# Own buffers for the group norm's inverse root, and the inversion's masked copies moved behind both chunk halves

## The chip, the cores and the metric

The kernel runs on one core of a Trainium2 chip. The metric is the device time of one execution in microseconds (us), given as the median of several runs. TensorE appears as PE (its weight loads as PEld), VectorE as DVE, ScalarE as ACT, GpSimd as POOL and SyncE as SP.

## The reference, cut to what matters

One decoder block of width 2048 over 512 positions in float32. A normalised input goes through one wide projection. A part of its columns feeds RWKV-7 time mixing (16 heads of 64), a part windowed attention, a part two gates. Both branches are projected, gated, summed and projected back; a gated convolution network of width 5632 follows. The change lies in the time mixing:

```python
h = rms_norm(x, norm1_g[l])
z = h @ w_in[l]
...
kk = kk / jnp.maximum(jnp.sqrt(jnp.sum(kk * kk, axis=-1, keepdims=True)), 1e-12)
...
def step(state, inp):
    r_t, k_t, v_t, w_t, ka_t, kb_t = inp
    sa = jnp.einsum('bhvk,bhk->bhv', state, ka_t)
    state = (state * w_t[:, :, None, :] + sa[..., None] * kb_t[:, :, None, :]
             + v_t[..., None] * k_t[:, :, None, :])
    y = jnp.einsum('bhvk,bhk->bhv', state, r_t)
    return state, y
...
mu = jnp.mean(y, axis=-1, keepdims=True)
var = jnp.mean(jnp.square(y - mu), axis=-1, keepdims=True)
y = ((y - mu) * lax.rsqrt(var + GN_EPS)).reshape(B, S, RW_DIM)
```

## The kernel before, in words

The wide projection is made in tiles of 128 columns. For each tile `project` takes 16 slices of the inner dimension with three matmuls each (lines 255, 256 and 257: high and low parts of input and weight), so a tile is 48 matmuls of 128x512 into a PSUM tile called `acc`. Weights come in four slices at a time: SP loads `raw` (line 237), ACT rounds it to `whi` (line 240), DVE makes the rest `wlo` (line 241). There are four buffers of each. These matmuls depend on nothing but weights, so they serve as filling for everything else on PE.

The 16 RWKV heads are worked on as 8 pairs. For a pair, `early` projects k, r and v and prepares them: it squares k, sums it per head on PE (line 327), takes an inverse root of those sums with `rsqrt_small` (lines 185 to 200, tiles `rq0` to `rq2`), transposes the result (line 330), copies it to `rsT` (line 332), sends it to DRAM and back as a row spread over partitions (`rsd`, line 334, and `rsb`, line 338, both on SP's queue), and multiplies k by it (line 552, `kk`). Beside this it makes the decay (lines 558 to 568) and the bonus (lines 584 to 593; line 591 is a matmul on PE that needs `lw` of line 589).

`late` then does the recurrence in 8 chunks of 64 positions. Lines 603 to 606 write the operands `BKK` and `BAR`, line 623 multiplies them, and lines 627 to 647 build what the inversion of a triangular 64x64 matrix starts from, in two halves `g` of four chunks each: a 2x2 start `X`, the matrix `AI` as a high part (ACT, line 209) and a low part (DVE, line 210), and two masked copies of `AI` called `BT` (line 647). Five levels follow on PE (lines 671 and 672; first with `AI`, then with `BT`). Then the chain runs through the chunks one after another: `psG` on PE (line 729), its copy `GY` on DVE (730), `psU` on PE (732), its two half copies `UV` on ACT (733) and DVE (734), `psS` on PE (738), the new state `SV` on DVE (742). The group norm ends it: sums, then `rsqrt_small` again (line 762) with the same two sets of buffers `rq`, and a product (line 763). `final` transposes the result (line 770), adds the bonus and stores it.

The program calls `late(p)`, `early(p + 1)`, `final(p)` and three gate tiles of the wide projection for each pair. The order that the engines get is made by a scheduler: it walks a heap of ready instructions by priority and by estimated times, and an instruction whose tile has no free buffer has to wait for it. Each engine then executes its list in order.

Of the kernel before, what the change touches and what calls it, by code (L numbers as in the profile page):

```python
# [8 lines left out]
F32 = mybir.dt.float32  # L9
# [9 lines left out]
P = 128  # L19
S = 512  # L20
NT = S // P
HD = 64
# [5 lines left out]
GN_EPS = 64e-5  # L28
# [106 lines left out]
def block_kernel(ctx: ExitStack, tc: tile.TileContext, d: Dims, a: dict, out: bass.AP):  # L135
# [47 lines left out]
    def col(nm, i=0):  # L183
        return pcol[:, PR[nm] + i : PR[nm] + i + 1]

    def rsqrt_small(pl, ss, scale, eps, mx=None):
        n = ss.shape[-1]
        tl = [pl.tile([P, 8], F32, name=f"rq{i}", tag=f"rq{i}", bufs=2)[:, :n] for i in range(3)]
        v, y, t = tl
        if mx is not None:  # L190
            dve.tensor_scalar(v, ss, mx, None, op0=ALU.max)
        else:
            dve.tensor_scalar(v, ss, scale, eps, op0=ALU.mult, op1=ALU.add)
        dve.tensor_scalar(t.bitcast(I32), v.bitcast(I32), 1, None, op0=ALU.logical_shift_right)
        dve.tensor_scalar(y.bitcast(I32), t.bitcast(I32), -1, 0x5F3759DF, op0=ALU.mult, op1=ALU.add)
        dve.tensor_scalar(v, v, -0.5, None, op0=ALU.mult)
        for _ in range(3):
            dve.tensor_tensor(t, y, y, op=ALU.mult)
            dve.tensor_tensor(t, t, v, op=ALU.mult)
            dve.scalar_tensor_tensor(y, t, 1.5, y, op0=ALU.add, op1=ALU.mult)  # L200
        return y
# [6 lines left out]
    def split(hi, lo, src, pin=free):  # L208
        pin(act.activation(hi, src, AF.Copy))
        pin(dve.tensor_tensor(lo, src, hi.bitcast(F32) if hi.dtype == F32R else hi, op=ALU.subtract))  # L210
# [67 lines left out]
    if True:  # L278
# [3 lines left out]
        with tc.tile_pool(name="x0_ps", bufs=6, space=PSUM) as ps0:  # L282
            ssum = p0.tile([P, NT], F32, name="ssum")
            HT = NT // 2
            for h in range(2):
                for t in range(h * HT, (h + 1) * HT):
                    sq = p0.tile([P, d.D], F32, name="sqx", tag="sqx", bufs=1)
                    act.activation(sq, xt[t], AF.Square, accum_out=ssum[:, t : t + 1])
                r = rsqrt_small(p0, ssum[:, h * HT : (h + 1) * HT], 1.0 / d.D, RMS_EPS)
                for t in range(HT):  # L290
                    dve.tensor_scalar(xt[h * HT + t], xt[h * HT + t], r[:, t : t + 1], None, op0=ALU.mult)
            first = {d.c_ka: [load_w(zt[d.c_ka][:, k0 : k0 + 4]) for k0 in range(0, min(NK, 12), 4)]}
            for h in range(2):
                hs = slice(h * HT * P, (h + 1) * HT * P)
                for k in range(NK):
                    ps = ps0.tile([P, HT * P], F32, name="ps_x", tag="x")
                    for t in range(HT):
                        pe.transpose(ps[:, t * P : (t + 1) * P], xt[h * HT + t][:, k * P : (k + 1) * P], ident)
                    g = col("n1g", k)
                    act.activation(xhi[:, k, hs], ps, AF.Identity, scale=g)  # L300
                    dve.scalar_tensor_tensor(xlo[:, k, hs], ps, g, xhi[:, k, hs].bitcast(F32), op0=ALU.mult, op1=ALU.subtract)  # L301
# [40 lines left out]
        with ExitStack() as pt:  # L342
# [16 lines left out]
            def qk_norm(acc, gain, dst, then=lambda: None):  # L359
                z = ap_.tile([P, S], F32, name="zq", tag="zq", bufs=3)  # L360
                dve.tensor_scalar(z, acc, gain, None, op0=ALU.mult)
                sq = ap_.tile([P, S], F32, name="sqq", tag="sqq", bufs=2)
                act.activation(sq, acc, AF.Square)
                ps = small()
                head_stats(ps, sq)
                rs = rsqrt_small(ap_, ps[:, 0 : 2 * NT], 1.0 / HD, RMS_EPS)
                rb = head_rows(ap_, small(), rs, bufs=2)
                finish()
                unscaled.append((dst, z, rb, then))
# [38 lines left out]
            for g in range(NHK):  # L408
# [7 lines left out]
                for n in range(NT):  # L416
# [15 lines left out]
                    st = ap_.tile([P, 4, GQ], F32, name="st", tag="st", bufs=2)  # L432
                    mx, es, den, rc = (st[:, i] for i in range(4))
# [33 lines left out]
        with ExitStack() as pr:  # L467
# [3 lines left out]
            wk = pr.enter_context(tc.tile_pool(name="wk", bufs=1, reuse_waits="tile"))  # L471
# [17 lines left out]
            def bulk():  # L489
                return blk.tile([P, S], F32, name="bulk", tag="bulk")  # L490
# [38 lines left out]
            def r3(ap, c=C):  # L529
                return ap.rearrange("p (n c) -> p n c", c=c)  # L530
# [5 lines left out]
            def early(p):  # L536
# [11 lines left out]
                ps = bulk()  # L548
                head_stats(ps, sq)
                rs = rsqrt_small(wk, ps[:, 0 : 2 * NT], None, None, mx=1e-24)  # L550
                rb = head_rows(wk, bulk(), rs, "lg")
                dve.tensor_tensor(kk, kk, rb, op=ALU.mult)
# [43 lines left out]
            def late(p, st):  # L596
# [17 lines left out]
                HN = NCH // 2  # L614

                def mb(nm, n, h=None):
                    m = K[nm] if h is None else K[nm][h[0] : h[1]]
                    return m.unsqueeze(1).to_broadcast([m.shape[0], n, m.shape[-1]])
# [11 lines left out]
                for g in range(2):  # L630
                    ns = slice(g * HN, (g + 1) * HN)
                    for h, (lo, hi) in enumerate(HV):
                        own = AB[lo:hi, ns, h]
                        (dve.tensor_copy if h else act.copy)(BX[lo:hi, ns, lo:hi], own)
                        dve.tensor_tensor(tt[lo:hi, ns], own, mb("m1", HN, (lo, hi)), op=ALU.mult)
                    dve.tensor_tensor(tt[:, ns], tt[:, ns], mb("istack", HN), op=ALU.add)
                    split(X[:, 0, ns], X[:, 1, ns], tt[:, ns])
                    ps = bulk().rearrange("p (n c) -> p n c", c=P)
                    for j in range(HN):
                        pe.transpose(ps[:, j], BX[:, g * HN + j], ident)  # L640
                    for h, (lo, hi) in enumerate(HV):
                        (dve.tensor_copy if h else act.copy)(BX[lo:hi, ns, lo:hi], tt[lo:hi, ns])
                    at_ = wk.tile([P, HN, P], F32, name="at_", tag="at_")
                    dve.scalar_tensor_tensor(at_, ps, SG, mb("idsg", HN), op0=ALU.mult, op1=ALU.add)
                    split(AI[:, 0, ns], AI[:, 1, ns], at_)
                    for i in range(2):
                        dve.tensor_tensor(BT[:, i, ns], AI[:, i, ns], mb("t1bd", HN), op=ALU.mult)
                for g in range(2):
                    ns = slice(g * HN, (g + 1) * HN)
# [76 lines left out]
                for n in range(NCH):  # L726
# [17 lines left out]
                    if n % HN == HN - 1:  # L744
                        ns = slice(n + 1 - HN, n + 1)
# [9 lines left out]
                st = wk.tile([P, 2, NCH], F32, name="st", tag="st")  # L755
# [3 lines left out]
                sq = wtile("gn")  # L759
                act.activation(sq, y, AF.Square)  # L760
                dve.reduce_sum(st[:, 1], r3(sq), axis=AX.X)
                rs = rsqrt_small(wk, st[:, 1], 1.0 / HD, GN_EPS)
                dve.tensor_tensor(y3, y3, rs.unsqueeze(2).to_broadcast([P, NCH, C]), op=ALU.mult)
                return ag, bon, y

# [18 lines left out]
            st = early(0)  # L784
            for p in range(NP):
                lt = late(p, st)
                if p + 1 < NP:
                    st = early(p + 1)
                final(p, lt)
                for _ in range(GATES_PER_PAIR * NK // 16):  # L790
                    emit_gate()
# [72 lines left out]
    with ExitStack() as pbb:  # L864
# [7 lines left out]
        g = {}  # L872
        for m, i in order:
            hi, lo, r0, n, gi = parts[i]
# [509 lines left out]
```

## Time and profile before

| | |
|---|---|
| three runs | 2885.1, 2887.93 and 2889.51 us, median 2887.93 |
| profiled execution, its own time | 2891.14 us |
| its span | 2889.4 us |
| PE busy | 2812.9 us (97%) |
| DVE busy | 1971.8 us (68%) |
| ACT busy | 1338.4 us (46%) |
| PE clock granted, mean | 0.988 |

The span is the part of the execution that the trace covers; 1.7 us of the time lie around it. A busy time is the sum of an engine's instructions without their overlaps. The granted clock says which share of TensorE's full clock it was given; times of matmuls grow where it is below 1.

### The profile page before, as it was taken

The page shows a single profiled execution, that of the slowest core. Times are in us where ns is not written, and L with a number is a line of the kernel's source. Part 1 is how long each engine was busy: PE and PEld are TensorE (multiplying, and loading weights), DVE is VectorE, ACT ScalarE, POOL GpSimd, SP SyncE. Part 2 cuts the span into 40 slices and gives each one's busy share as a digit, 9 for nine tenths or more (in the row PEclk, how much of TensorE's full clock was granted, in tenths as well). Part 3 has the DMA queues.
Part 4 walks back from the last instruction along what each step waited for, and adds up shares of the span by engine and source line. Part 5 has one row for each costly group of instructions (what it writes and reads, how often), then busy time and mean ns, then how long its engine had stood idle before and what let it go on. Part 6 is the DMA issues. An engine that isn't in the chain of part 4 may idle for free.

```text
span 2889.4 us, 45975 instructions
## 1 busy us (share of the span) xinstructions
PE 2812.9 (97%) x17478; PEld 2417.0 (84%) x17478; DVE 1971.8 (68%) x3423; ACT 1338.4 (46%) x2258; POOL 226.0 (8%) x299
## 2 busy tenths in 40 slices
PE   7999999999999999999999899999999999999999
PEld 5777777777777777888888899999999999888887
DVE  5577667757767766544668787777777777655555
ACT  4345445435445435322456455554555545544444
POOL 0001000000000000111001001111010100000000
PEclk9999999999999999999999999999999999999999
DMA  7855766575575575788777788888888988877775
GB/s 216 224 153 156 183 171 163 146 178 140 140 181 144 137 177 142 237 261 252 276 264 209 217 223 227 229 241 232 231 225 231 241 230 226 312 241 245 255 256 189
DMA packets 223725, 607.03 MB, mean 210 GB/s; under 512 B 24448, under 2 KB 44560, under 8 KB 222480
## 3 DMA queue, kind: packets, MB, share of 16 engines
q1 hardware_dynamic: 156096, 432.64, 46.2%
q0 software_dynamic: 36064, 132.14, 23.9%
q10 hardware_dynamic: 31344, 39.31, 4.0%
q8 instruction: 137, 2.24, 0.3%
q14 instruction: 84, 0.69, 0.1%
HBM read 554.38 MB, written 174.40 MB: 252 GB/s over the span
## 4 chain that ended last, share of the span: by engine, by line
PE 87%; DVE 7%; ACT 2%; DMA 2%; issue 1%; ACTq 0%; SPq 0%; DVEq 0%; POOLq 0%
PE X L1085 16%; PE X L952 11%; PE acc L255 10%; PE acc L257 10%; PE acc L256 9%; PE Y L952 9%; PE Y L1085 8%; PE Z L1085 4%; PE psS L738 1%; DMA rsb<-rsd 1%; PE psG L729 1%; PE bulk L623 1%; PE bulk L534 1%; PE bulk L671 1%; DVE wlo L241 1%
## 5 line engine op out<-in xcount | busy, mean ns | idle before, releaser
L257 PE MATMUL acc<-xhi,wlo 128*128 128x512 f32 x1152 | 466.5, 405 | 7.8 <-DVE wlo L241 7.8
L255 PE MATMUL acc<-xhi,whi 128*128 128x512 f32 x1152 | 467.7, 406 | 1.9 <-DVE xlo L301 1.9
L256 PE MATMUL acc<-xlo,whi 128*128 128x512 f32 x1152 | 468.5, 407 | 0.0
L240 ACT ACTIVATE whi<-raw 128x512 fp32r<-128x512 f32 x352 | 220.9, 630 | 467.6 <-PE acc L256 331.0
L945 DVE TENSOR_TENSOR wlo<-raw,whi 128x1024 fp32r<-128x1024 f32 x210 | 256.9, 1224 | 205.3 <-ACT whi L944 202.2
L241 DVE TENSOR_TENSOR wlo<-raw,whi 128x512 fp32r<-128x512 f32 x352 | 240.9, 689 | 173.4 <-ACT whi L240 145.6
L944 ACT ACTIVATE whi<-raw 128x1024 fp32r<-128x1024 f32 x210 | 222.7, 1061 | 289.4 <-PE X L952 150.3
L1085 PE MATMUL X<-b,whi 128*128 128x256 f32 x1472 | 271.0, 285 | 2.3 <-DVE u L1105 0.9
L1085 PE MATMUL X<-t,whi 128*128 128x256 f32 x1408 | 260.3, 285 | 8.8 <-DVE u L1105 8.3
L1068 DVE TENSOR_TENSOR wlo<-raw,whi 128x1024 fp32r<-128x1024 f32 x176 | 214.9, 1222 | 78.2 <-ACT whi L1067 77.6
L257 PEld LDWEIGHTS acc<-xhi,wlo 128*128 128x128 f32 x1152 | 220.0, 191 | 50.9 <-DVE wlo L241 8.7
L1085 PE MATMUL Y<-t,whi 128*128 128x256 f32 x1408 | 257.6, 283 | 0.0
L255 PEld LDWEIGHTS acc<-xhi,whi 128*128 128x128 f32 x1152 | 219.5, 191 | 43.9 <-issue 2.2
L256 PEld LDWEIGHTS acc<-xlo,whi 128*128 128x128 f32 x1152 | 219.7, 191 | 38.9 <-issue 1.6
L1067 ACT ACTIVATE whi<-a 128x1024 fp32r<-128x1024 f32 x132 | 139.3, 1056 | 213.8 <-DVE a L1061 211.5
L1085 PEld LDWEIGHTS X<-b,whi 128*128 128x128 f32 x1472 | 231.2, 193 | 3.1 <-issue 2.4
L1085 PEld LDWEIGHTS X<-t,whi 128*128 128x128 f32 x1408 | 222.0, 194 | 9.4 <-DVE u L1105 5.8
L1085 PEld LDWEIGHTS Y<-t,whi 128*128 128x128 f32 x1408 | 220.1, 192 | 0.0
L1085 PE MATMUL X<-b,wlo 128*128 128x256 f32 x736 | 209.6, 285 | 2.3 <-DVE wlo L1068 2.3
L1068 DVE TENSOR_TENSOR wlo<-a,whi 128x1024 fp32r<-128x1024 f32 x132 | 161.6, 1225 | 67.7 <-ACT whi L1067 67.0
L1085 PE MATMUL X<-t,wlo 128*128 128x256 f32 x704 | 200.7, 285 | 0.5 <-DVE wlo L1068 0.5
L1085 PE MATMUL Y<-t,wlo 128*128 128x256 f32 x704 | 199.4, 283 | 0.0
(335 smaller groups left out, 5779.2 us busy)
## 6 DMA issues: line engine op xcount, KB each, us to landing
raw<-in_w_up_dram SPq DMA_DIRECT2D x180, 512.0 KB
raw<-in_w_z_dram SPq DMA_DIRECT2D x288, 256.0 KB
s_dn<-in_w_dn_dram POOLq DMA_DIRECT2D x88, 512.0 KB, 6.6
raw<-in_w_up_dram POOLq DMA_DIRECT2D x88, 512.0 KB, 8.6
raw<-s_dn SPq DMA_DIRECT2D x88, 512.0 KB
raw<-in_w_dn_dram SPq DMA_DIRECT2D x66, 512.0 KB
a<-in_w_up_dram SPq DMA_DIRECT2D x48, 512.0 KB
s_dn<-in_w_dn_dram SPq DMA_DIRECT2D x44, 512.0 KB
```

The source lines that it names most:

```text
L240: act.activation(hi, raw, AF.Copy)
L241: dve.tensor_tensor(lo, raw, hi.bitcast(F32), op=ALU.subtract)
L255: pe.matmul(acc, whi[:, j], xhi[:, k], start=first, stop=False)
L256: pe.matmul(acc, whi[:, j], xlo[:, k], start=False, stop=False)
L257: pe.matmul(acc, wlo[:, j], xhi[:, k], start=False, stop=last)
L534: pe.matmul(ps, w[:, i], ads[:, i], start=i == lo, stop=i == hi - 1)
L944: act.activation(whi, wr, AF.Copy)
L945: dve.tensor_tensor(wlo, wr, whi.bitcast(F32), op=ALU.subtract)
L952: pe.matmul(dst, l[:, q, ts], r[:, es], start=fst and j == 0, stop=lst and j == 2, skip_group_check=True)
L1067: pin(act.activation(hi, t, AF.Copy))
L1068: pin(dve.tensor_tensor(lo, t, hi.bitcast(F32), op=ALU.subtract))
L1085: pin(pe.matmul(ps, l[:, k], r[:, k], start=start and k + i == 0, stop=last and i == 2, skip_group_check=True))
```

## The change

The inverse root of the group norm gets tiles `rg0` to `rg2`, two of each, in place of a share of `rq0` to `rq2`. The loop that makes the masked copies `BT` becomes a loop of its own behind the loop over both halves.

```diff
-    def rsqrt_small(pl, ss, scale, eps, mx=None):
+    def rsqrt_small(pl, ss, scale, eps, mx=None, tag="rq"):
         n = ss.shape[-1]
-        tl = [pl.tile([P, 8], F32, name=f"rq{i}", tag=f"rq{i}", bufs=2)[:, :n] for i in range(3)]
+        tl = [pl.tile([P, 8], F32, name=f"{tag}{i}", tag=f"{tag}{i}", bufs=2)[:, :n] for i in range(3)]
...
                     split(AI[:, 0, ns], AI[:, 1, ns], at_)
+                for g in range(2):
+                    ns = slice(g * HN, (g + 1) * HN)
                     for i in range(2):
                         dve.tensor_tensor(BT[:, i, ns], AI[:, i, ns], mb("t1bd", HN), op=ALU.mult)
...
-                rs = rsqrt_small(wk, st[:, 1], 1.0 / HD, GN_EPS)
+                rs = rsqrt_small(wk, st[:, 1], 1.0 / HD, GN_EPS, tag="rg")
```

No instruction is added or taken away. From line 647 on, line numbers of the changed kernel are 2 higher. The lists of the engines differ from the first inversion up to the projections behind the last pair; ahead of that and behind it they are the same.

First place, DVE, the k of the next pair. Before, its list from the copy `rsT` to the product `kk` that needs the row back from DRAM:

```order
L332 COPY rsT<-bulk 8x128
L561 TENSOR_SCALAR lw<-lw 128x512
L606 TENSOR_TENSOR BAR<-rz,Et 64x8x64 x2
L583 TENSOR_SCALAR k_6188<-lw,half 128x512
L241 TENSOR_TENSOR wlo<-raw,whi 128x512
L584 TENSOR_TENSOR k_6188<-k_6188,kz 128x512
L585 TENSOR_SCALAR lw<-lw 128x512
L552 TENSOR_TENSOR kk<-kk,rsb 128x512
```

Now, the same stretch and what stands behind it:

```order
L332 COPY rsT<-bulk 8x128
L744 SCALAR_TENSOR_TENSOR SV<-SV,ee,psS 64x64 x2
L561 TENSOR_SCALAR lw<-lw 128x512
L732 COPY GY<-psG 128x128
L241 TENSOR_TENSOR wlo<-raw,whi 128x512
L736 COPY UV<-psU 64x64
L744 SCALAR_TENSOR_TENSOR SV<-SV,ee,psS 64x64 x2
L583 TENSOR_SCALAR k_6188<-lw,half 128x512
L584 TENSOR_TENSOR k_6188<-k_6188,kz 128x512
L732 COPY GY<-psG 128x128
L552 TENSOR_TENSOR kk<-kk,rsb 128x512
L585 TENSOR_SCALAR lw<-lw 128x512
```

The stretch stood behind the chain and the group norm of the pair before; now it stands among the chain's second to fourth chunk, and the next row is the fourth chunk's `UV` copy (L736). The rest of the next pair's preparation (lines 587, 589, 593 and 603 to 606, 11 instructions) follows between the steps of the remaining chunks.

Second place, PE, the same stretch, with the chain's matmuls (`psG`, `psU`, `psS`) and the filling (`acc`). Before:

```order
L330 MATMUL bulk<-ident,rq_5987 8x128
L558 MATMUL bulk<-wl,thw 128x128 x4
L255 MATMUL acc<-xhi,whi 128x512
L256 MATMUL acc<-xlo,whi 128x512
L257 MATMUL acc<-xhi,wlo 128x512
L255 MATMUL acc<-xhi,whi 128x512
L256 MATMUL acc<-xlo,whi 128x512
L565 MATMUL bulk<-cst,lw 128x128 x4
L534 MATMUL bulk<-ads,wl 128x512
```

Now:

```order
L330 MATMUL bulk<-ident,rq_5987 8x128
L558 MATMUL bulk<-wl,thw 128x128 x2
L740 MATMUL psS<-UV,W_2914 128x64 x2
L558 MATMUL bulk<-wl,thw 128x128 x2
L257 MATMUL acc<-xhi,wlo 128x512
L255 MATMUL acc<-xhi,whi 128x512
L731 MATMUL psG<-SV,BAR 128x64 x2
L256 MATMUL acc<-xlo,whi 128x512
L257 MATMUL acc<-xhi,wlo 128x512
L565 MATMUL bulk<-cst,lw 128x128 x2
L734 MATMUL psU<-GY,BX 128x128
L565 MATMUL bulk<-cst,lw 128x128 x2
```

After these stand L534, `psS`, four `acc`, `psG`, five `acc`, `psU`, four `acc` and the fourth chunk's `psS`. Line 591, which stood behind 28 `acc` and ahead of the next pair's first matmuls of line 623, now stands in the fifth chunk.

Third place, DVE, the start of the inversion, from the low part of the first half's `AI` on. Before:

```order
L210 TENSOR_TENSOR AI<-at__6499,AI 128x512
L647 TENSOR_TENSOR BT<-AI,cst 128x512 x2
L636 TENSOR_TENSOR tt<-tt,cst 128x256
L644 SCALAR_TENSOR_TENSOR at__6519<-bulk,cst 128x512
L210 TENSOR_TENSOR XIW<-tt,XIW 128x256
L642 COPY BX<-tt 64x4x64
L545 TENSOR_SCALAR kk<-kz,par 128x512
L210 TENSOR_TENSOR AI<-at__6519,AI 128x512
L647 TENSOR_TENSOR BT<-AI,cst 128x512 x2
L241 TENSOR_TENSOR wlo<-raw,whi 128x512
```

Now (line 649 is what line 647 was):

```order
L210 TENSOR_TENSOR AI<-at__6499,AI 128x512
L636 TENSOR_TENSOR tt<-tt,cst 128x256
L644 SCALAR_TENSOR_TENSOR at__6517<-bulk,cst 128x512
L642 COPY BX<-tt 64x4x64
L649 TENSOR_TENSOR BT<-AI,cst 128x512
L210 TENSOR_TENSOR XIW<-tt,XIW 128x256
L649 TENSOR_TENSOR BT<-AI,cst 128x512
L210 TENSOR_TENSOR AI<-at__6517,AI 128x512
L649 TENSOR_TENSOR BT<-AI,cst 128x512 x2
L241 TENSOR_TENSOR wlo<-raw,whi 128x512
```

Two of the four masked copies still stand ahead of the second half's low part, but the tile `at_` that both parts of `AI` are made from comes ahead of them. The instruction of line 545 has gone to a later place. Ahead of the first instruction of line 627 two instructions of line 241 now stand in a row, and when PE comes to line 623 four weight slices of filling that it has not used are ahead of that point in DVE's list, where it was two; between the last matmul of line 623 and the first ones with `BT` PE has 46 matmuls of filling where it had 34.

## The prediction

> **What bounds the kernel now.** I read the page first, then busy time by stage, then PE's own list of waits, then single pairs in order of time.
>
> ```profile
> span 2889.4 us, 45975 instructions
> PE 2812.9 (97%) x17478; PEld 2417.0 (84%) x17478; DVE 1971.8 (68%) x3423; ACT 1338.4 (46%) x2258; POOL 226.0 (8%) x299
> ```
>
> PE works almost throughout, so only time in which PE waits, or runs at a lower clock, can be won. The next view has one row for each stretch: length, busy time of PE, PEld, DVE, ACT and POOL, then PE's granted clock. The first row is six periods of the pair loop (from the product `kk` of the second pair to that of the eighth), the second the last pair, the third what follows.
>
> ```profile
> 434.80:1078.70 643.90, 615.45 (x3840) 476.67 (x3839) 436.70 (x1083) 284.67 (x629) 50.30 (x67) 0.97 0.63 156
> 1078.70:1180.00 101.30, 98.59 (x620) 75.96 (x619) 68.48 (x160) 44.78 (x102) 5.47 (x7) 0.98 0.60 151
> 1180.00:1387.00 207.00, 207.00 (x915) 171.41 (x914) 103.75 (x171) 60.10 (x99) 27.69 (x40) 1.00 0.85 269
> ```
>
> Behind the pairs PE is full and at clock 1.00: nothing is lost there. In the six periods PE idles 643.90 - 615.45 = 28.4 us, and a clock of 0.97 costs up to 0.03 x 643.90 = 19.3 us; the last pair adds 2.7 and 2.0. About 4 of the clock's part falls on time in which PE waits anyway (an estimate), so about 48 us is all that the order of the pair loop can give back. PE's waits in both stretches together (us, times, longest):
>
> ```profile
> PE bulk L591 <- DVE lw L589: 13.1, 7, 2.8
> PE acc L257 <- DVE wlo L241: 7.8, 5, 2.2
> PE bulk L672 <- DVE AI L210: 3.5, 4, 0.9
> PE bulk L671 <- ACT AI L209: 2.9, 4, 0.7
> ```
>
> Two places, then: line 591 in the next pair's preparation (13.1 us), and the start of the inversion (the other three, 14.2 us). The clock falls right behind them; here the pair around 650, where PE sits idle for 2.01 us ahead of line 591 at 653.15, and its inversion:
>
> ```profile
> 652.00:656.00 4.00, 2.85 (x7) 1.75 (x8) 3.76 (x7) 0.17 (x2) 0.81 (x1) 0.66 0.39 48
> 656.00:660.00 4.00, 4.00 (x14) 2.52 (x14) 2.96 (x6) 1.49 (x4) 0.00 (x0) 0.92 0.58 135
> ```
>
> ```profile
> 653.15 1.94 PE L591 MATMUL bulk<-lw,cst 128*128 128x512 f32 x2 [2.01 <-DVE lw L589]
> ```
>
> ```profile
> 672.00:676.00 4.00, 1.80 (x10) 1.41 (x11) 3.83 (x9) 3.08 (x8) 0.00 (x0) 0.72 0.07 21
> 676.00:680.00 4.00, 4.00 (x25) 2.99 (x24) 2.10 (x5) 1.15 (x3) 0.00 (x0) 0.50 0.74 196
> ```
>
> The first drop costs (0.34 + 0.08) x 4 = 1.7 us, the second (0.28 + 0.50) x 4 = 3.1 us, the idle part included. At the second DVE is busy 3.83 of 4 us: there PE waits for DVE's throughput, not for a transfer.
>
> **The buffers.** Before, both inverse roots drew on one ring of two `rq` sets, the group norm's first in program order, and the next pair's k could not be normalised until the chain was over. By the order it now starts in the chain's second chunk. That moves 16 wide DVE instructions per pair (lines 552, 561, 583 to 589, 593, 603 to 606), four wide ACT ones and line 591 into the chain. Work is neither added nor removed, so the wait at line 591 as it stands goes: -13.1 us. What was it waiting for? DVE's list says it:
>
> ```profile
> 640.87 0.27 DVE L332 COPY rsT<-bulk 8x128 f32<-8x128 f32 x1
> ...
> 647.63 0.42 DVE L585 TENSOR_SCALAR lw<-lw 128x512 f32<-128x512 f32 x1
> 649.85 0.69 DVE L552 TENSOR_TENSOR kk<-kk,rsb 128x512 f32<-128x512 f32 x1 [1.79 <-DMA rsb<-rsd]
> ```
>
> The row goes out to DRAM and comes back in 649.85 - 640.87 = 8.98 us, and DVE sits idle for the last 1.79. The trip stays as long as it is. On SP's queue its three transfers still stand behind every weight load that has a free buffer, as before, so I leave it at that. The question is what is queued behind `kk` now: the `UV` copy of the fourth chunk, for which PE's `psS` waits. I walk PE's new list from line 330 to that `psS`, with starts from these rows:
>
> ```profile
> 621.33 0.59 PE L729 MATMUL psG<-SV,BAR 128*128 128x64 f32 x4
> 621.73 0.48 PE L256 MATMUL acc<-xlo,whi 128*128 128x512 f32 x1
> ...
> 622.51 0.38 PE L732 MATMUL psU<-GY,BX 128*128 128x128 f32 x2
> 622.65 0.48 PE L256 MATMUL acc<-xlo,whi 128*128 128x512 f32 x1
> 622.96 0.40 PE L257 MATMUL acc<-xhi,wlo 128*128 128x512 f32 x1
> 623.20 0.40 PE L255 MATMUL acc<-xhi,whi 128*128 128x512 f32 x1
> ...
> 623.91 0.66 PE L738 MATMUL psS<-UV,W 128*128 128x64 f32 x4
> 624.38 0.48 PE L255 MATMUL acc<-xhi,whi 128*128 128x512 f32 x1
> ```
>
> ```profile
> 640.40 0.27 PE L330 MATMUL bulk<-ident,rq 128*8 128x128 f32 x1
> ...
> 641.33 0.47 PE L255 MATMUL acc<-xhi,whi 128*128 128x512 f32 x1
> ...
> 642.72 1.16 PE L565 MATMUL bulk<-cst,lw 128*128 128x128 f32 x8
> ...
> 644.18 0.79 PE L257 MATMUL acc<-xhi,wlo 128*128 128x512 f32 x1
> ```
>
> Lines 330 and 558 take 0.93, lines 565 and 534 1.46; two each of `psG` (0.40), `psU` (0.14) and `psS` (0.47) take 2.0; 17 matmuls of filling at 0.23 take 3.9; seven times the filling resumes after other work and its first matmul takes 0.31 instead (0.6); small waits 0.2. Sum 9.1 us from line 330 to `psS`. On DVE `rsT` starts 0.47 after line 330 and `kk` 8.98 after that, at 9.45; `kk`, line 585 and the copy `UV` then take some 1.3, to 10.75. So PE waits 1.65 us in this pair. DVE's idle time before `kk` in the six periods is smaller on average:
>
> ```profile
> L552 DVE TENSOR_TENSOR kk<-kk,rsb 128x512 f32<-128x512 f32 x6 | 4.2, 692 | 9.8 <-DMA rsb<-rsd 9.8
> ```
>
> 9.8 / 6 = 1.6 against 1.79, so I take 1.5 us for each of the seven pairs: +10.3. The bounds are 0 (the scheduler's filling covers it) and 2.8 (the longest wait at line 591). The wait is moved, not removed.
>
> The other 15 wide instructions stand between chain steps. From `psG` to `psU` PE has 622.51 - 621.33 = 1.18 us, and `GY` needs 0.9 of it; the same walk through all eight chunks, with the new fillings (3 to 7 matmuls where a wide instruction stands, 3 to 5 before), leaves each step 0 to 0.3 us of slack. I put 0.3 us per pair on steps that miss it: +2.1.
>
> **The masked copies.** A pair's four copies stay 2.6 us of DVE work, since one takes 0.64:
>
> ```profile
> 668.37 1.29 DVE L647 TENSOR_TENSOR BT<-AI,cst 128x512 f16<-128x512 f16 x2
> ...
> 671.61 0.48 DVE L545 TENSOR_SCALAR kk<-kz,par 128x512 f32<-128x512 f32 x1
> ```
>
> Two came ahead of the second half's `at_`; now none does, which gives ACT its part of `AI` 1.2 us earlier. DVE's low part still has two ahead of it and gains only line 545 (0.4). More comes from the order around: 46 matmuls of filling where there were 34 up to the first with `BT`, 12 x 0.23 = 2.8 us of cover, and two more weight slices ready. The mean wait was 14.2 / 6 = 2.4 us per inversion, less than the 2.8 + 0.4 that now stand against it. So -14.2, and -0.7 in the last pair. ACT, with eight copies of line 665 in a row, can still hold back the first use of `BT`; for that I put back 0.5 (between 0 and 1.0) for seven pairs: +3.5.
>
> **The clock.** Its 19.3 - 4 + 2.0 = 17.3 us go with the waits behind which it fell. A wait of 1.5 us in the chain can make it fall again: between 0 and 1.7 us each; I take a third, 0.6, since waits are shorter than the 2.01 us above: +4.2. The Trainium skill ("TensorE: Matmul & The Clock Gate", Part 1) has the clock halved only after an idle window of about 3.4 us. The trace disagrees: 2.01 us were followed by 0.66. By that page no wait of the new order would touch the clock, and the 4.2 would be 0.
>
> **The sum.** -13.1 + 10.3 + 2.1 - 14.2 - 0.7 + 3.5 - 17.3 + 4.2 = -25.2 us. The profiled execution took 2891.14 (span 2889.4), so it would take 2866; the median of the runs, 2887.93, is 3.2 lower, which makes 2863.
>
> **The rivals.**
> - The trip is covered by filling and the clock stays up: without 10.3 and 4.2 it is -40, 2848. For it: PE records no wait inside the chain today. The Trainium skill's page named above would have the clock's half of this. Against: the 9.1 us that I count are shorter than the trip. Chance 0.13.
> - The trip costs its full 2.8 us and takes the clock down by 1.7 each time: (2.8 - 1.5 + 1.1) x 7 = 17 us worse, -8: 2880. Chance 0.13.
> - Slower: the wide instructions make the chain late. DVE takes its list in order (all behind `kk` waited the 1.79 us too), and a 0.69 us instruction that has just begun when `psG` or `psU` is ready delays the copy by half of it on average, 0.33. If PE has to wait for all 16 of them, 5.3 us per pair, 37 us in seven instead of 2.1: +10, 2898. It decides from (25 + 2) / (7 x 16) = 0.24 us per instruction. Against it: the filling in the list is longer where these instructions stand. Chance 0.15.
> - The change does nothing, because the waits only trade places: within 6 us. Chance 0.06, since the order shows that lines 552 and 591 did move.
>
> **How the numbers follow.** The forecast has the remaining 0.53. A measurement of this kernel can tell about 0.2% (6 us) from no change. Faster by more than that are the forecast, the first rival and most of the second (0.53 + 0.13 + 0.10), within it the rest of the second and the last, 0.09 in all, slower 0.15. The range reaches from the first rival (2848) to 2884, past the second, and leaves out the slower case and part of no change, 0.2.
>
> **What would show it.** Right: line 591 without a wait in PE's list; `psS` waiting for `UV`, seven times, for 1 to 2 us, behind an idle DVE before `kk`; lines 257, 671 and 672 together under 5 us; period of the pairs near 103 us instead of 643.9 / 6 = 107.3; clock 0.99 in the loop. Wrong: waits at `psG`, `psU` and `psS` in most chunks (then the third rival), or a clock that stays at 0.97.

## The result, and the profile after

| | before | after |
|---|---|---|
| median of the runs | 2887.74 us (2885.1 to 2889.51, 4 runs) | 2839.88 us (2838.36 to 2841.2, 4 runs) |
| profiled execution, its own time | 2891.14 us | 2838.93 us |
| its span | 2889.4 us | 2837.2 us |
| PE clock granted, mean | 0.988 | 0.997 |

The ratio is 0.9836, with a 95% interval of 0.9824 to 0.9848: 48 us faster. The forecast was 25 us faster with a range of 2848 to 2884, so the direction was right and the size lay outside the range. Measured again later, the changed kernel took 2838.03 us against 2888.87.

The kernel after, the first two lines of the page:

```profile
span 2837.2 us, 45968 instructions
PE 2781.8 (98%) x17478; PEld 2407.4 (85%) x17478; DVE 1983.6 (70%) x3423; ACT 1339.2 (47%) x2258; POOL 225.4 (8%) x299
```

To say where the time went one needs stretches that hold the same work. From the first matmul of line 558 to the first one behind the projections (line 952 before, 954 after), PE executes 6085 matmuls in both kernels. Busy time by stretch, the kernel before first (length, busy PE, PEld, DVE, ACT and POOL, clock, DMA share, GB/s):

```profile
316.70:1387.00 1070.30, 1035.91 (x6085) 815.01 (x6085) 687.91 (x1605) 441.56 (x941) 92.67 (x126) 0.98 0.67 179
```

```profile
315.40:1336.20 1020.80, 1008.38 (x6085) 807.06 (x6085) 699.43 (x1605) 441.74 (x941) 92.08 (x126) 1.00 0.71 187
```

The stretch is 49.5 us shorter. PE's idle time fell from 34.4 to 12.4 us (22.0), and the same matmuls are busy for 27.5 us less. Six periods of the pair loop, as in the first row of the prediction's second view:

```profile
400.50:988.80 588.30, 581.09 (x3804) 462.14 (x3802) 444.66 (x1082) 281.27 (x624) 48.91 (x66) 1.00 0.67 167
```

A period is 588.3 / 6 = 98.05 us instead of 107.3, and the clock no longer falls. Not all of this is gain: the six periods hold 36 matmuls fewer than before (3804 against 3840), which at the walk's 0.23 us each are 1.4 us a period. PE's waits between 300 and 1180 us (us, times, longest):

```profile
PE bulk L673 <- DVE XIW L210: 5.4, 14, 0.6
PE bulk L772 <- DVE yc L765: 1.8, 8, 0.2
PE bulk L623 <- DVE bon L593: 1.6, 1, 1.6
PE bulk L623 <- DVE BAR L606: 0.5, 1, 0.5
PE psS L740 <- DVE UV L736: 0.2, 1, 0.2
```

Line 591 is gone from the list, as forecast. `psS`, which was to wait seven times for 1 to 2 us, waits once for 0.2. The prediction's pair, on DVE and on PE:

```profile
687.33 0.28 DVE L332 COPY rsT<-bulk 8x128 f32<-8x128 f32 x1
...
694.48 0.68 DVE L552 TENSOR_TENSOR kk<-kk,rsb 128x512 f32<-128x512 f32 x1
```

```profile
686.86 0.27 PE L330 MATMUL bulk<-ident,rq 128*8 128x128 f32 x1
...
695.90 0.57 PE L740 MATMUL psS<-UV,W 128*128 128x64 f32 x4
```

From line 330 to the fourth chunk's `psS` PE takes 695.90 - 686.86 = 9.04 us; the walk had said 9.1. But `kk` comes 694.48 - 687.33 = 7.15 us after `rsT`, with no idle time ahead of it in its row, so the row was back by then. The prediction had 8.98. In five of the other six pairs it is 7.14 to 7.17 us; in the last it is 7.57, with 0.33 us of DVE's waiting for the row.

### The profile page after: what moved, and what is told of

Its sections match the earlier page's. It is cut to its first block, busy times and chain, and to the rows that moved or that the text cites. A ratio compares the mean times of both kernels' runs of the same rounds, so it can differ in the third digit from the quotient of the medians.

```text
span 2837.2 us, 45968 instructions
## 1 busy us (share of the span) xinstructions
PE 2781.8 (98%) x17478; PEld 2407.4 (85%) x17478; DVE 1983.6 (70%) x3423; ACT 1339.2 (47%) x2258; POOL 225.4 (8%) x299
## 4 chain that ended last, share of the span: by engine, by line
PE 87%; DVE 5%; ACT 3%; DMA 2%; issue 1%; ACTq 0%; SPq 0%; POOL 0%; DVEq 0%; POOLq 0%
PE X L1087 17%; PE X L954 11%; PE acc L256 9%; PE acc L255 9%; PE acc L257 9%; PE Y L954 9%; PE Y L1087 8%; PE Z L1087 4%; DVE wlo L241 1%; PE psS L740 1%; DMA raw<-in_w_up_dram 1%; PE psG L731 1%; PE bulk L623 1%; PE bulk L673 1%; PE mi L457 1%
## 5 line engine op out<-in xcount | busy, mean ns | idle before, releaser
L255 PE MATMUL acc<-xhi,whi 128*128 128x512 f32 x1152 | 461.9, 401 | 1.9 <-DVE xlo L301 1.9
L256 PE MATMUL acc<-xlo,whi 128*128 128x512 f32 x1152 | 461.7, 401 | 0.0
```

What stands on the lines that cost most here:

```text
L255: pe.matmul(acc, whi[:, j], xhi[:, k], start=first, stop=False)
L256: pe.matmul(acc, whi[:, j], xlo[:, k], start=False, stop=False)
```

## The experiments

**Which half does it?** Each half of the change alone. First the buffers, with the two lines of `rsqrt_small` that take the name:

```diff
...
-                rs = rsqrt_small(wk, st[:, 1], 1.0 / HD, GN_EPS)
+                rs = rsqrt_small(wk, st[:, 1], 1.0 / HD, GN_EPS, tag="rg")
```

> The group norm's own buffers without the move of the copies. The prediction's steps: -13.1 (line 591) + 10.3 (psS waits for the trip) + 2.1 (chain) - 5.8 (line 591's share of the clock: 4 of the 12 half-clock stretches of 3.4 us in the loop, of 17.3) + 4.2 = -2.3 us, so about 2885. Theory A (the trip is shorter here than before because no accumulating sum is issued beside it, so that the 9.0 us of PE work cover it): no psS waits, -13.1 - 5.8 = -19, about 2869, trip of rsT to kk 7.2 us or less; the waits at the start of the inversion (14.2 us) stay.

Measured: 2843.07 us against 2889.06, ratio 0.9836 (0.9818 to 0.9854). Both expectations missed: this half has nearly the whole gain. Its trace between 315 and 1340 us, the largest of PE's waits, and the stretch of the 6085 matmuls:

```profile
PE bulk L671 <- DVE XIW L210: 3.4, 8, 0.6
```

```profile
315.10:1340.70 1025.60, 1015.71 (x6085) 807.50 (x6085) 698.57 (x1605) 434.98 (x941) 91.86 (x126) 1.00 0.70 186
```

The waits for `wlo` and `AI` (14.2 us before) are no longer in its list, although the copies stand where they stood; 3.4 us for `XIW` are the largest that is left. The stretch is 4.8 us longer than in the changed kernel, but the two profiled executions have the same span, 2837.2 us. In the medians 2843.07 stands against 2839.88 and, in the later runs, 2838.03, with intervals that overlap. So what the copies' move adds to the buffers is not shown; by the medians it is 3 to 5 us.

Then the copies, with both roots on one ring:

```diff
+                for g in range(2):
+                    ns = slice(g * HN, (g + 1) * HN)
                     for i in range(2):
                         dve.tensor_tensor(BT[:, i, ns], AI[:, i, ns], mb("t1bd", HN), op=ALU.mult)
```

> The move of the masked copies with the two roots still on one ring. The prediction's steps: -14.2 - 0.7 + 3.5 - 11.5 (the other 8 of 12 half-clock stretches) = -22.9, about 2865. Theory A with the waits that the changed kernel's trace has at the inversion (5.4 us) gives -14.9 + 5.4 - 11.5 = -21, about 2867; line 591 keeps its 13.1 us and the trip its 8.8 us with the sum beside it. Rival: the halves work on each other (the clock falls at the inversion because it fell 20 us earlier, or the other way round); then the two gains do not add up to the 48 of both together within 6 us.

Measured: 2889.08 us against 2889.06, ratio 1.0001 (0.9989 to 1.0014). Nothing, where both expectations had over 20 us. PE's waits between 316 and 1385 us:

```profile
PE bulk L591 <- DVE lw L589: 15.2, 7, 4.4
PE acc L257 <- DVE wlo L241: 14.3, 6, 3.7
```

`AI` has left the list but for 1.0 us, as the move intended. In its place the filling's `wlo` makes PE wait for 14.3 us instead of 7.8: the wait traded places. The two gains, 46 and 0 us, add up to the 48 of both within the 6 us that the second expectation allows, so nothing shows that the halves work on each other.

**Why the new order inside the inversion gained nothing.** Two rows each for the pair at 600 us before and at 680 us after: from the chain's first `psG` to its end, and from there to the first matmul of the inversion's levels.

```profile
599.60:630.50 30.90, 30.90 (x177) 24.74 (x174) 14.07 (x40) 7.75 (x19) 2.73 (x4) 1.00 0.70 175
630.50:669.84 39.34, 37.12 (x171) 28.02 (x170) 31.24 (x83) 15.87 (x33) 3.08 (x5) 0.96 0.53 128
```

```profile
679.70:711.60 31.90, 31.90 (x189) 25.97 (x186) 23.85 (x67) 9.26 (x22) 1.61 (x2) 1.00 0.64 157
711.60:740.06 28.46, 28.20 (x135) 22.22 (x134) 23.15 (x59) 12.47 (x28) 4.08 (x6) 1.00 0.76 189
```

Read DVE's column (the third count). Before, DVE was busy for 14 of 31 us in the chain and then had 31 us of work to do while PE waited for it. Now 24 us lie in the chain and 23 behind it. If that amount is what counts, more of it must cost time before and not after. Each masked copy made twice, in both kernels:

```diff
-                        dve.tensor_tensor(BT[:, i, ns], AI[:, i, ns], mb("t1bd", HN), op=ALU.mult)
+                        for _ in range(2):
+                            dve.tensor_tensor(BT[:, i, ns], AI[:, i, ns], mb("t1bd", HN), op=ALU.mult)
```

> The kernel before with each masked copy made twice: 2.6 us more of VectorE's work per pair at the start of the inversion, nothing else. Theory D (TensorE waits there for the amount of VectorE's work between kk and the inversion, not for the place of one instruction): +2.6 us in each of six or seven pairs, +15 to +18, and up to 6 more by the clock, 2903 to 2913. Rival P (the prediction: what counts is which instruction stands ahead of AI's low part): the two extra copies of the first half that stand ahead of it delay it by 1.3 us, +8 to +9, 2896 to 2898.

> The changed kernel with each masked copy made twice. Theory D: VectorE has slack at the inversion since its wide instructions of the preparation went into the chain; the residual wait there is 5.4 us in 14 stops of 0.1 to 0.6, and the 2.6 us more per pair are covered by filling in part: 0 to +6, 2840 to 2846. If VectorE were as tight there as before, +15 to +18, 2855 to 2858.

Measured: before, 2910.4 us against 2889.78, +20.6 (ratio 1.0075, 1.006 to 1.0089), as theory D had it and not rival P. After, 2835.44 us, ratio 0.981 (0.9793 to 0.9827): none lost, which is a little under theory D's 2840 to 2846; by the medians 3 to 4 us are won, with an interval that overlaps the changed kernel's. PE's waits in the doubled kernel before (316 to 1408 us), then after (316 to 1334 us):

```profile
PE acc L257 <- DVE wlo L241: 22.0, 8, 3.7
PE bulk L591 <- DVE lw L589: 18.6, 7, 3.4
```

```profile
PE bulk L674 <- DVE XIW L210: 0.7, 2, 0.4
```

With the copies in their old place the extra 2.6 us per pair came out as waits, 14.2 us more at `wlo` and 5.5 more at line 591. In the changed kernel DVE had room, and the scheduler put more filling ahead of the levels, 51 matmuls where it was 46: the wait for `XIW` fell from 5.4 to 0.7 us.

So the waits were for the amount of DVE's work, set against the filling that PE has meanwhile. PE's lists show the filling, between the last matmul of line 623 and the first with `BT`. The kernel before has 34 matmuls there in four pairs, and waits of about 3 us in each of them; 41 in one, with 2.15 us; 48 to 51 in the other three, with none of these waits. The copies' move alone makes it 30 in three pairs, each with a wait of 3.69 us; the buffers alone make it 44 in seven pairs, and both halves 46 in all eight. So the buffers did two things at once: they moved DVE's work into the chain, and with the new order 10 matmuls of filling, 2.3 us, came ahead of the levels. From the last matmul of line 623 to the first with `BT` a pair with 34 took 16.4 to 16.9 us, and a pair now takes 14.7 to 14.8, although it holds more filling. How much of the gain is the one and how much the other, no run separates.

**Why the trip is shorter.** The accumulating sums are a background job: SP copies half a megabyte of weights from DRAM to DRAM (line 230), GpSimd's queue adds another (line 231). Around the trip, GpSimd's queue before and after:

```profile
641.80 0.95 POOL L231 DMA_DIRECT2D s_dn<-in_w_dn_dram  x1 [10.53 <-DMA s_dn<-in_w_dn_dram]
```

```profile
683.10 0.81 POOL L231 DMA_DIRECT2D s_dn<-in_w_dn_dram  x1 [10.13 <-DMA s_dn<-in_w_dn_dram]
697.59 0.81 POOL L231 DMA_DIRECT2D s_dn<-in_w_dn_dram  x1 [13.68 <-DMA s_dn<-in_w_dn_dram]
```

Before, the sum started 0.9 us after `rsT` (640.87), right on the trip. After, one starts 4.2 us ahead of `rsT` and the next 3.1 us behind the start of `kk` (694.48). From issue to landing these sums take 5.9 us (median in the changed kernel's loop), so the first of them still covers the trip's first 1.7 us. To test it, the sums of the pair loop were set one weight slice later, with no other instruction of PE, DVE or ACT moved:

```diff
+            wp["n"] += 2
             st = early(0)
             for p in range(NP):
...
+            wp["n"] -= 2
```

> The changed kernel with the accumulating sums of the pair loop one weight slice later in the queue; the orders of TensorE, VectorE and ScalarE are those of the changed kernel, instruction for instruction. One slice stands between a sum's first half and the trip, so that the second half (the accumulating one on GpSimd's queue) is issued about when rsd is. Theory A (the trip's length is set by what is transferred beside it): the trip takes 8.5 to 9 us instead of 7.2, psS waits for UV 1 to 2 us in each of the seven pairs, and the time is 8 to 14 us above the changed kernel's, 2848 to 2854, more if the clock falls behind these waits. Rival B (the trip is shorter for the engines' new order, whatever is transferred beside it): 7.2 us as in the changed kernel, and its time within 3 us.

Measured: 2848.84 us, ratio 0.9858 (0.9839 to 0.9876), 9.0 us above the changed kernel's first median and 10.8 above its second. The sum, the trip and the wait of the same pair, and all such waits:

```profile
689.90 0.81 POOL L231 DMA_DIRECT2D s_dn<-in_w_dn_dram  x1 [9.15 <-DMA s_dn<-in_w_dn_dram]
```

```profile
691.37 0.28 DVE L332 COPY rsT<-bulk 8x128 f32<-8x128 f32 x1
...
699.96 0.69 DVE L552 TENSOR_TENSOR kk<-kk,rsb 128x512 f32<-128x512 f32 x1 [1.35 <-DMA rsb<-rsd]
```

```profile
PE psS L740 <- DVE UV L736: 8.8, 7, 1.8
```

The sum now starts 1.5 us ahead of `rsT` (1.2 to 1.9 in the seven pairs), the trip takes 8.59 us, and PE waits at `psS` in all seven pairs, 1.26 us on average. By the forecast's own terms this trip gives 0.47 + 8.59 + 1.3 - 9.1 = 1.26 us. So the forecast's wait comes back when one transfer is put in another place.

The other way round: the kernel before, with its order, but no sums in the loop. They come behind it, four and twelve times as often, so the whole time (3098.01 us, one run) says nothing, and only the loop is read.

```diff
+            wp["step"] = 10 ** 9
             st = early(0)
...
-            wp["step"] = 4
+            wp["step"] = 1
...
-    wp["step"] = 12
+    wp["step"] = 1
```

> The kernel before with no accumulating sums in the pair loop (they come behind it, three and twelve times as often, so only the loop is read, not the whole time). In the loop the orders of TensorE, VectorE and ScalarE are those of the kernel before, instruction for instruction. Theory A (the transfers beside the trip set its length): the trip falls from 8.8 us to 7.5 or less, DVE's idle time before kk from 1.6 us a pair to under 0.3, the wait at line 591 from 13.1 us to 2 to 5, and the clock no longer falls there. The waits at the start of the inversion (14.2 us) stay, as VectorE's work there is the same. Rival B (the trip is long for the engines' order): line 591 keeps over 10 us.

The six periods, three of PE's waits in them, and one trip; the two rows of line 591 are all that is left of the 11.1 us that it had in the six periods before (13.1 with the seventh pair):

```profile
430.21:1057.42 627.21, 608.32 (x3833) 472.34 (x3833) 436.17 (x1085) 284.55 (x628) 9.56 (x18) 0.98 0.29 78
```

```profile
PE acc L257 <- DVE wlo L241: 7.8, 5, 2.1
...
PE bulk L591 <- ACT whi L240: 0.5, 1, 0.5
PE bulk L591 <- DVE lw L589: 0.3, 1, 0.3
```

```profile
632.35 0.27 DVE L332 COPY rsT<-bulk 8x128 f32<-8x128 f32 x1
...
639.44 0.69 DVE L552 TENSOR_TENSOR kk<-kk,rsb 128x512 f32<-128x512 f32 x1
```

In this trace `kk` starts 7.09 to 7.45 us after `rsT`, in six of seven pairs without idle time. A period is 627.21 / 6 = 104.5 us, 2.8 less than before, of which 0.3 are seven matmuls fewer. The wait for `wlo` stayed at 7.8 us, as did those for `AI` at 3.5 and 2.9. So the two losses are separate: the trip cost some 2.5 us a pair, with its share of the clock, and the waits at the inversion are not its work.

Two things stand beside this. SP's weight loads are another candidate, for they too stand otherwise around the trip: before, one starts 2.6 us ahead of `rsT` and one 0.1 us behind it, now one 1.5 us ahead. But the run without sums has the old loads and a short trip, and the run with the later sums the new loads and a long one. And a sum beside the trip does not lengthen it every time: in the first of the seven pairs before, the sum started 0.24 us behind `rsT` and the trip took 7.51 us, against 8.18 to 9.77 in the other six.

**Longer trips.** The row fetched in pieces of 256 bytes:

```diff
-                sync.dma_start(rb[h * HD : (h + 1) * HD], src[h : h + 1].to_broadcast([HD, S]))
+                sync.dma_start(rb[h * HD : (h + 1) * HD], src[h : h + 1].to_broadcast([HD, S]),
+                               max_dma_last_dim=4 * S if bufs > 1 else 256)
```

> The changed kernel with the row's two loads back from DRAM in pieces of 256 bytes (eight to each partition's 2 KB) in the pair loop; the orders of TensorE, VectorE and ScalarE are unchanged. It lengthens the trip alone, by an unknown amount. If the 9.0 us between line 330 and psS are all that covers the trip, PE waits at psS for (trip - 7.3) us in each of seven pairs and the time grows by 7 times that, with no clock loss as long as a wait is under 2 us (prediction: a third of 1.7 us per wait of 1.5). If the cover is longer than counted, a trip of up to 9 us costs nothing. A wait of 2 us or more at psS should show a granted clock under 0.9 behind it, as at line 591 before.

Measured: 2840.92 us (ratio 0.983, 0.9811 to 0.9849), `kk` 7.15 to 7.19 us after `rsT` in six pairs and 7.79 in one, where the sum is 2.5 us ahead instead of 4.1 to 4.7. In the six DVE does not wait for the row, so what the pieces add, if anything, is hidden, and this run decides nothing. One more hop did lengthen the trip:

```diff
             sync.dma_start(rd, sm)
+            if tag == "lg" and bufs == 1:
+                r2 = dram.tile([2 * NT, P], F32, name="rse", tag="rse", bufs=4)
+                sync.dma_start(r2, rd)
+                rd = r2
```

> The changed kernel with one more hop of the row from DRAM to DRAM in the trip of the pair loop; it lengthens the trip by 2 to 3 us. If the 9 us of PE work from line 330 to psS are all the cover (theory A): trip 9.2 to 10.2, PE waits at psS for 1.9 to 2.9 us in each of seven pairs, 13 to 20 us, and the clock falls behind those over 1.8 us, 1 to 1.7 us each: +14 to +32, 2854 to 2872. If the scheduler, which sees the hop, sets more filling ahead of it, less: 0 to +10.

Measured: 2837.56 us, ratio 0.9821 (0.9803 to 0.9838), and no wait at `psS` at all. The scheduler estimates the hop too and sets `kk` one chunk later:

```profile
694.75 0.23 DVE L740 COPY UV<-psU 64x64 f32<-64x64 f32 x1
...
697.34 0.68 DVE L556 TENSOR_TENSOR kk<-kk,rsb 128x512 f32<-128x512 f32 x1
```

The copy `UV` of the fourth chunk now stands ahead of `kk`, which comes 10.8 us after `rsT` and waits for nothing. If place is all that matters, it must also hold off the later sums:

> Both at once: the sums one weight slice later (alone +9 us over the changed kernel: psS waits of 8.8 us in seven) and the extra hop (alone no loss: with it kk stands one chunk later in VectorE's list). If the loss of the later sums was only that kk stands where the scheduler's length for the trip puts it, the hop's later place holds it although the real trip is longer still: no waits at psS, 2835 to 2841. If the accumulating sum costs in another way (weight slices that come late, SP's queue), 2846 to 2852 as without the hop.

Measured: 2841.18 us, ratio 0.9834 (0.982 to 0.9847), against 2838.03 for the changed kernel on the same chip, at the upper end of the first expectation. The waits at `psS` fell from 8.8 us to this:

```profile
PE psS L744 <- DVE UV L740: 1.0, 2, 0.8
```

**The changed kernel again**, as a measure for small differences:

> The changed kernel itself, beside the two below on one chip: 2838 to 2843, the loop as in its first profile (idle 7 us in six periods, clock 1.00), for comparing with small differences.

Measured: 2838.03 us (2835.87 to 2839.97), 587.9 us for the six periods.

**The price of wide DVE instructions in the chain.** Lines 603 to 606 made twice, eight more per pair:

```diff
-                    dve.tensor_tensor(BKK[hs, :, lo:hi], kb3[hs], Ei3[hs], op=ALU.mult)
...
+                    for _ in range(2):
+                        dve.tensor_tensor(BKK[hs, :, lo:hi], kb3[hs], Ei3[hs], op=ALU.mult)
...
```

> The changed kernel with lines 603 to 606 made twice: eight more wide VectorE instructions of 0.68 us (5.4 us) per pair, in the chain. By the prediction's slower rival, each of them would cost 0.33 us of a copy that PE waits for: 8 x 7 x 0.33 = +18 us, 2858. If VectorE has slack in the chain (it is busy 76% of the loop in the changed kernel), 0 to +5, 2840 to 2845; a few waits at psG or psU would then show, under 0.5 us a pair.

Measured: 2850.95 us, ratio 0.9868 (0.9852 to 0.9883), 12.9 above the changed kernel: between the two expectations, so the place has to be read. PE's waits up to 406 us, the first pair, which has no chain ahead of it, and then behind it:

```profile
PE bulk L624 <- DVE BAR L607: 4.1, 1, 4.1
```

```profile
PE bulk L674 <- DVE XIW L210: 4.8, 12, 0.6
PE bulk L773 <- DVE yc L766: 4.0, 8, 0.9
PE psS L741 <- DVE UV L737: 0.2, 1, 0.2
```

And busy time of the two stretches, this kernel and then the changed one on the same chip:

```profile
320.00:407.00 87.00, 78.10 (x509) 61.85 (x507) 63.54 (x143) 41.69 (x90) 5.67 (x7) 0.94 0.54 138
407.00:1004.00 597.00, 587.59 (x3829) 467.02 (x3829) 476.38 (x1132) 283.34 (x626) 48.87 (x66) 1.00 0.67 167
```

```profile
320.00:402.00 82.00, 79.16 (x537) 62.67 (x535) 60.92 (x139) 42.63 (x92) 5.82 (x7) 1.00 0.64 161
402.00:990.00 588.00, 580.55 (x3800) 461.73 (x3799) 444.93 (x1081) 281.40 (x624) 48.89 (x66) 1.00 0.67 167
```

The first pair takes 5 us longer and gets 28 matmuls less done (6.5 us at 0.23), at a clock of 0.94: 11.5 us. In the six periods 9 us are added, but 29 more matmuls are done in them (6.8 us), so about 2 us are the price of 48 extra instructions in the chain, 0.05 us each. The slower rival had put 0.33 on each and needed 0.24. These are two single executions, 17.5 us apart in their spans, where the medians are 12.9 apart; the other 4 us lie behind these stretches, and their cause is open.

## Why the prediction was right or wrong

- **What bounds the kernel: right, the size in part by luck.** Only PE's idle time and clock in the pair loop could be won, "about 48 us", and 49.5 came back. But the 48 were 31.1 of idle time and 17.3 of clock, and what came back are 22.0 of idle time and 27.5 of busy time.
- **Where the forecast fell short.** Its terms add up to 12.1 us of waits and 13.1 of clock. The waits gave 9.9 more, nearly all of it the trip's 10.3; the busy time gave 14.4 more, of which 4.2 are the clock that the trip's waits were to cost again, and the rest is a clock term that was too small.
- **Line 591, -13.1: right.** The wait is gone. Its cause was the trip, as DVE's list had shown: without the sums it shrank to 0.8 us in the old order too.
- **The trip, +10.3: wrong, and this is the step that failed.** "The trip stays as long as it is." The walk on PE was right (9.04 us against 9.1), and so was the price: with a trip of 8.59 us in the later sums the waits came to 8.8 us in seven pairs. But the trip did not keep its length. It was read at 8.98 us with half a megabyte being added to DRAM beside it, and the change took `kk` away from that transfer. The prediction looked at SP's weight loads, "as before", and passed over GpSimd's queue, although the sum's row lies on the trip. The 7.17 us or less of six pairs stand under the limit of 9.1 - 0.47 - 1.3 = 7.3 with little to spare, and the 7.57 of the last pair gave the one wait of 0.2 us. The first rival, at a chance of 0.13, came nearest with its 2848, but for another reason (more filling).
- **The chain's slack, +2.1: too much.** One wait of 0.2 us; 0.05 us for each further wide instruction.
- **The masked copies, -14.2 - 0.7 + 3.5: the size nearly right, the cause wrong.** 5.4 us of new waits remain at line 673, so -9.5 instead of -11.4, and 1.8 us at line 772 were not foreseen. The 2.8 us of cover that the prediction counted, 46 matmuls of filling for 34, are there. But it counted them with the copies' move, and they come with the buffers: 44 with these alone, 30 in three pairs with the copies alone, which gained nothing. The row with DVE busy for 3.83 of 4 us had said that PE waits for DVE's throughput there; the work that the buffers take from there was left out of the sum.
- **The clock, -17.3 + 4.2: both too cautious.** The same matmuls are busy for 27.5 us less. By the clock's column the loop had lost at most 19.3 + 2.0 = 21.3; what the other 6 us are (matmuls that start slowly behind a wait are one candidate) stays open. The 4.2 were nothing here: no wait in the six periods is over 0.6 us now. "The clock falls right behind them" holds for four of the seven waits at line 591, and not for the longest (the last section has the rows).
- **The slower rival: refuted** by the one wait of 0.2 us in the chain, and by the run with doubled wide instructions. **"The waits only trade places": true of the copies' move made alone,** which gained nothing and turned waits for `AI` into waits for `wlo`.

## What to carry to other kernels

Before a wait is moved, look at what else is on the DMA queues while it lasts, on every engine's queue: a round trip through DRAM that was measured beside a big transfer can be shorter elsewhere, and a background transfer can be moved off it. Where an engine is busy all through a stretch that another waits for, a new order inside the stretch may only decide who waits, as here. What helped was less of its work in the stretch and more filling for the engine that waits, and one small buffer that ties two stages together can be what prevents both. Run both halves of a change alone: here one half gained nearly everything, and the other nothing by itself.

## What the runs showed of the hardware

The same trip of 4 KB to DRAM and back as a row took 7.17 us or less in six of seven pairs (7.57 in the other) with an accumulating sum issued about 4 us ahead, and 8.24 to 9.25 us with one issued 1.2 to 1.9 us ahead, at the same order of all three compute engines. At the old order it took 8.18 us or more in six of seven pairs with sums, and 7.45 or less without any. The Trainium skill ("DMA: Bandwidth & Descriptors", Latency and other measured facts) has access to DRAM at 0.2 us on average and 2 us at high load, and a smaller fixed cost where the load is lighter; this agrees in direction with the 0.7 us or more that the load cost here in all pairs but the one of 7.51 us, over one transfer out and two back, though how much of it is access and how much is waiting for a DMA engine the runs do not show.

The clock: in the run with the later sums, seven waits of 0.8 to 1.8 us in the chain were followed by one fall of the clock, behind the longest, 1.84 us. PE there, and the two stretches of 4 us around it:

```profile
901.04 0.66 PE L740 MATMUL psS<-UV,W 128*128 128x64 f32 x4 [1.84 <-DVE UV L736]
```

```profile
899.00:903.00 4.00, 2.15 (x12) 1.67 (x11) 3.17 (x8) 0.39 (x1) 0.00 (x0) 0.94 0.23 61
903.00:907.00 4.00, 4.00 (x15) 3.07 (x14) 2.56 (x6) 0.22 (x1) 0.00 (x0) 0.63 0.18 37
```

The other six, of 0.8 to 1.5 us at the same place, cost no clock. The Trainium skill ("TensorE: Matmul & The Clock Gate", Part 1) speaks of an idle window of about 3.4 us; here 1.84 us of idle time were enough once, and 2.01 us in the kernel before. But length alone does not decide. A wait of 2.80 us in the kernel before, and one of 3.12 us at the same line in the run with the copies alone, cost no clock; the first of them, and the 4 us around its end:

```profile
545.42 1.10 PE L591 MATMUL bulk<-lw,cst 128*128 128x512 f32 x2 [2.80 <-DVE lw L589]
```

```profile
545.00:549.00 4.00, 3.52 (x11) 1.75 (x12) 3.93 (x7) 1.51 (x4) 0.00 (x0) 1.00 0.00 0
```

What else decides, no run here shows.
